# Token projections of a hybrid SSD and attention block: TensorE taken in source order, transposes one tile behind, the scan in three portions

## The chip, the cores and the metric

The kernel runs on one core of a Trainium2 chip. The metric is the device time of one execution in microseconds (us); lower is better. The engines are named as in the profile: PE is TensorE (matrix products and transposes), DVE is VectorE, ACT is ScalarE, POOL is GpSimd, SP is SyncE, which here only issues DMAs.

## The reference

Two layers over 256 context and 1024 latent tokens of width 1024 (10 tiles of 128 tokens). Each layer projects the normalised input once and splits the result between three branches:

```
p = split_proj((rmsnorm(h, g_pre) * (1 + sc) + sh)  w_in)   # xbc z dt | gq gk gv gg | dq dk dv dg
# A  SSD: conv on xbc, then a chunked scan forward and backward, chunks of 128
y_diag = einsum('bcqhn,bcshn,bchqs,bcshp->bcqhp', cc, bc, lmat, xd)
states = einsum('bcshn,bcsh,bcshp->bchpn', bc, decay_states, xd)
y_off  = einsum('bcqhn,bchpn,bcqh->bcqhp', cc, states_in, exp(a_cum))
y_s = rmsnorm((y_f + y_b + x * d_skip) * silu(z), norm_g)
# B  grouped-query attention: 4 query and 2 key heads of 64, rmsnorm and rotary on q and k
# C  differential attention: 8 query and 8 key heads of 32, rotary, 4 value heads of 64
h = h + gt * rmsnorm(concat([y_s, y_g * silu(gg), y_d * silu(dg)])  w_out, g_post)
```

The last layer drops the context's output.

## The kernel before, in words

All matrix products that need full precision are split: each operand is a high and a low part, and a product is three matmuls. Between the convolution and the attention of each layer lies the region that is touched here (about 206 to 602 us in the first layer, 1273 to 1625 us in the second).

**The token projections.** `tok_chunk` (L938 to L1000) runs five column chunks in the order 0 (gate z), 1 (differential q and k), 3 (differential v, 256 wide), 2 (grouped q, k, v, called gqa below), 4 (the attention's gate). A chunk loads 8 weight blocks (`wf`), splits them into `wh` and `wl` (9 buffers each), and then takes the 10 tiles of tokens. A tile is 8 blocks times 3 matmuls, 24 matmuls (L958, L959, L960) into one of two PSUM buffers `prj`. What follows a tile is by chunk: a gate (tanh, ACT, and one DVE step); or, for q and k, a copy `raw`, the norm `gqa_norm`, the rotary `rope`, the split `st` (L834 and L128), the transposes `qps` on PE (L841), a copy `tt` and the stores.

**The scan.** `scan` (L754) is a generator that walks the 10 chunks forward (`c`) and backward (`cb`). It is advanced beside chunks 0, 1 and 3, 1.3 portions for a tile that is 512 wide. `state_step` scales x on POOL (`xs`, L708), multiplies (`stp`, L714) and updates a state; `y_off` multiplies with the state (`po`, L726), and DVE scales the result into `yt` (L728). For each forward chunk a decay matrix is made in the buffer `ab` (16 DVE steps, `Exp`, 16 more steps, and a POOL product, L782), and its product is `pd` (L790). `ab`, `xs`, `yt` and `yp` have one buffer each.

**The finish.** `finish` (the gated norm with the transposes `ytp`, L744) runs beside chunks 2 and 4. `split_wout` prepares the output weights (`wos`) and stores them; some of these run before this region, the rest beside chunk 2.

**What sets the order.** The program is written in one order, and the framework then orders each engine's queue by a simulated timeline with priorities by position in the source. So PE's queue before is not the source's: an instruction that the timeline has not ready is put later, and matmuls of a following tile are taken first. Each engine then works strictly down its queue and waits on semaphores. SP issues nearly all DMAs in its queue's order, so a store that waits for its data holds the loads behind it.

The tables for the rotary (`cosg`, `sing`, and the products `Ckg`, `Cqg`, L930 and L931) are made at the start of the region.

Of the kernel before, what the change touches and what calls it, by code (L numbers as in the profile page):

```python
# [18 lines left out]
P = 128  # L19
KT = 8  # L20
# [47 lines left out]
def block_kernel(ctx: ExitStack, tc: tile.TileContext, tok, cvec, wmod, pack,  # L68
# [360 lines left out]
    for l in range(DEPTH):  # L429
# [275 lines left out]
        def state_step(c, dr, xb, S, first):  # L705

            xs = sp.tile([P, 2, 256], F32, name="xs", tag="xs")
# [14 lines left out]
        def y_off(c, dr, bc, S):  # L722

            po = xpp.tile([P, 2, 256], F32, name="po", tag="po")
            for g in range(2):
                TE.matmul(po[:, g], bc[g], S[:, g], start=True, stop=True)  # L726
            yt = sp.tile([P, 512], F32, name="yt", tag="yt")
            V.tensor_tensor(heads(yt), heads(po.rearrange("p g x -> p (g x)")), per_head(eacs, dr, c), op=ALU.mult)  # L728
            return yt

        def finish(c, fp, nb=2):
# [4 lines left out]
            SY.dma_start(zt, d_z[c])  # L736
            V.tensor_tensor(y, y, zt, op=ALU.mult)
# [3 lines left out]
            V.tensor_scalar(y, y, rr, None, op0=ALU.mult)  # L741
            pt = trp.tile([P, 4, P], F32, name="ytp", tag="tr")
# [9 lines left out]

        def scan():
# [3 lines left out]
            for c, cb in enumerate((1, 0, 9, 8, 7, 6, 5, 4, 3, 2)):  # L757
                xb = sp.tile([P, 2, 384], F32, name="xbf", tag="xb", bufs=2)
                SY.dma_start(xb, d_xb[c])
                if c >= t0:  # L760
                    ab = sp.tile([P, 2, 8, P], F32, name="ab", tag="ab")
                    SY.dma_start(ab, d_acs[:, c].unsqueeze(0).to_broadcast([P, 2, 8, P]))
                    bc = sp.tile([P, 4, P], F32, name="bct", tag="bct", bufs=2)
                    SY.dma_start(bc, d_bc[:, :, cs(c)].rearrange("i p t -> p i t"))
                    pg = xpp.tile([P, 2, P], F32, name="gp", tag="gp")
                    for g in range(2):
                        TE.matmul(pg[:, g], bc[:, 2 * g], bc[:, 2 * g + 1], start=True, stop=True)
                    gf = sp.tile([P, 2, 2, P], F32, name="gf", tag="gf")
                    V.tensor_tensor(gf[:, 0], pg, mge.unsqueeze(1).to_broadcast([P, 2, P]), op=ALU.mult)
                    V.tensor_tensor(gf[:, 1], pg, mle.unsqueeze(1).to_broadcast([P, 2, P]), op=ALU.mult)  # L770
                    D, W = ab[:, 0], ab[:, 1]
                    for h in range(8):
                        V.tensor_scalar(D[:, h], D[:, h], acs[:, 0, c, h:h + 1], None, op0=ALU.subtract)
                        V.scalar_tensor_tensor(D[:, h], W[:, h], acs[:, 1, c, h:h + 1], D[:, h],
                                               op0=ALU.subtract, op1=ALU.min)
                    S_.activation(D, D, AF.Exp)
                    yield
                    for h in range(8):
                        S_.activation(W[:, h], gf[:, 0, h // 4], AF.Copy, scale=dts[:, 0, c, h:h + 1])
                        V.scalar_tensor_tensor(W[:, h], gf[:, 1, h // 4], dts[:, 1, c, h:h + 1], W[:, h],  # L780
                                               op0=ALU.mult, op1=ALU.add)
                    G.tensor_tensor(W, W, D, op=ALU.mult)  # L782
                    y = sp.tile([P, 512], F32, name="y", tag="y", bufs=2)
                    G.tensor_tensor(y.rearrange("p (g h d) -> p g h d", g=2, h=4),
                                    xb[:, :, 0:256].rearrange("p g (h d) -> p g h d", h=4),
                                    pc("dskip").rearrange("p (g h) -> p g h", g=2).unsqueeze(3)
                                    .to_broadcast([P, 2, 4, 64]), op=ALU.mult)
                    pd = xpp.tile([P, 8, 64], F32, name="pd", tag="pd")
                    for h in range(8):
                        TE.matmul(pd[:, h], W[:, h], xb[:, h // 4, h % 4 * 64:h % 4 * 64 + 64],  # L790
                                  start=True, stop=True)
                    V.tensor_tensor(y, pd.rearrange("p h d -> p (h d)"), y, op=ALU.add)
                    if c:
                        yt = y_off(c, 0, (bc[:, 1], bc[:, 3]), Sf)
                        G.tensor_tensor(y, yt, y, op=ALU.add)
                    if c in half:
                        yt = sp.tile([P, 512], F32, name="yp", tag="yp")
                        SY.dma_start(yt, d_yp[c])
                        G.tensor_tensor(y, yt, y, op=ALU.add)
                    whole = c in half or c == 1  # L800
                    half.add(c)
                    SY.dma_start((d_ys if whole else d_yp)[c], y)
                    yield
                if c != NT - 1:
                    state_step(c, 0, xb, Sf, c == 0)
                xb = sp.tile([P, 2, 384], F32, name="xbb", tag="xb", bufs=2)
                SY.dma_start(xb, d_xb[cb])
                if c and cb >= t0:
                    ct = sp.tile([P, 2, P], F32, name="ct", tag="ct")
                    SY.dma_start(ct, d_bc.rearrange("(g b) p t -> b p g t", b=2)[1][:, :, cs(cb)])  # L810
                    yt = y_off(cb, 1, (ct[:, 0], ct[:, 1]), Sb)
                    if cb in half:
                        y = sp.tile([P, 512], F32, name="y", tag="y", bufs=2)
                        SY.dma_start(y, d_yp[cb])
                        G.tensor_tensor(y, yt, y, op=ALU.add)
                        SY.dma_start(d_ys[cb], y)
                    else:
                        half.add(cb)
                        SY.dma_start(d_yp[cb], yt)
                if cb != 2:  # L820
                    state_step(cb, 1, xb, Sb, c == 0)
                yield

# [85 lines left out]
        with pool("rot") as rp, pool("tokc", 2) as ck:  # L909
            rd = rp.tile([P, 3, 8, 16], F32, name="rd")  # L910
            cosd, sind, nsind = rd[:, 0], rd[:, 1], rd[:, 2]
            cosg = ck.tile([P, 8, 32], F32, name="cosg", tag="st", bufs=2)
            sing = ck.tile([P, 8, 32], F32, name="sing", tag="st", bufs=2)
            SY.dma_start(rd, roped.rearrange("a p t c -> p a t c"))
            SY.dma_start(cosg, ropeg[0])
            SY.dma_start(sing, ropeg[1])
            gain = {}
            for n, sc in (("qg", 64 ** -0.5), ("kg", 1.0)):
                gn = rp.tile([P, 64], F32, name=f"gn{n}")
                V.tensor_scalar(gn, pc(n), sc, None, op0=ALU.mult)  # L920
                gain[n] = gn

            tab = {}
            for n in ("kg", "qg"):
                c_ = rp.tile([P, 8, 2, 32], F32, name=f"C{n}")
                s_ = rp.tile([P, 8, 2, 32], F32, name=f"S{n}")
                for hf in range(2):
                    ga = gain[n][:, hf * 32:hf * 32 + 32].unsqueeze(1).to_broadcast([P, 8, 32])
                    gb = gain[n][:, 32 - hf * 32:64 - hf * 32].unsqueeze(1).to_broadcast([P, 8, 32])
# [692 lines left out]
```

## Times and profile before

| | us |
|---|---|
| three runs, median (lowest, highest) | 2074.26 (2069.14, 2074.6) |
| the profiled execution's own time | 2063.46 |
| its span | 2061.6 |
| PE busy | 1806.6 (88%) |
| DVE busy | 1428.5 (69%) |
| POOL busy | 1211.7 (59%) |
| ACT busy | 1041.5 (51%) |

The mean granted clock of PE over the span is 0.937. "Busy" is the union of the instructions on an engine; PE's matmuls overlap, so the time from one start to the next is the price of one. A bracket behind an instruction, [1.90 <-DVE th], is the idle time of its engine just ahead of it and what released it. In a window, idle PE is its length less its busy time, and a PEclk under 1.00 says that a part of it ran at the lower of the clock's two levels, 1.2 in place of 2.4 GHz.

### The profile page before, as it was taken

The page shows a single profiled execution, that of the slowest core. Times are in us where ns is not written, and L with a number is a line of the kernel's source. Part 1 is how long each engine was busy: PE and PEld are TensorE (multiplying, and loading weights), DVE is VectorE, ACT ScalarE, POOL GpSimd, SP SyncE. Part 2 cuts the span into 40 slices and gives each one's busy share as a digit, 9 for nine tenths or more (in the row PEclk, how much of TensorE's full clock was granted, in tenths as well). Part 3 has the DMA queues.
Part 4 walks back from the last instruction along what each step waited for, and adds up shares of the span by engine and source line. Part 5 has one row for each costly group of instructions (what it writes and reads, how often), then busy time and mean ns, then how long its engine had stood idle before and what let it go on. Part 6 is the DMA issues. An engine that isn't in the chain of part 4 may idle for free. (4 is left out here: it accounts for less than half of the span.)

```text
span 2061.6 us, 30333 instructions
## 1 busy us (share of the span) xinstructions
PE 1806.6 (88%) x9936; PEld 1471.4 (71%) x9936; DVE 1428.5 (69%) x3286; ACT 1041.5 (51%) x1955; POOL 1211.7 (59%) x1135
## 2 busy tenths in 40 slices
PE   4899989899879999988988799888899899989895
PEld 3677777787668667876775487777777777878783
DVE  4777566766538776698866578468656588788954
ACT  3445233334437775766654345234244477777661
POOL 3626245747616676777755326466567378787761
PEclk9899999899999999998989899999999999999897
DMA  9157546776786788786656138667766866557545
GB/s 290 47 170 271 152 165 191 236 235 176 222 259 198 245 263 257 234 256 202 211 191 214 63 102 280 226 183 231 244 202 204 260 185 192 157 155 237 161 152 205
DMA packets 359998, 418.57 MB, mean 203 GB/s; under 512 B 38753, under 2 KB 252833, under 8 KB 359841
## 3 DMA queue, kind: packets, MB, share of 16 engines
q1 hardware_dynamic: 359840, 416.64, 65.1%
q8 instruction: 78, 1.28, 0.3%
q14 instruction: 80, 0.65, 0.1%
HBM read 282.18 MB, written 134.38 MB: 202 GB/s over the span
## 5 line engine op out<-in xcount | busy, mean ns | idle before, releaser
L128 POOL TENSOR_TENSOR pl<-pf,ph 128x512 fp32r<-128x512 f32 x283 | 373.6, 1325 | 189.0 <-DVE ph L1391 69.7
L1241 DVE TENSOR_SCALAR_CACHE_REDUCE pt<-sc 128x512 f32<-128x512 f32 (+1 forms) x600 | 334.2, 587 | 78.5 <-PE sc L1239 63.4
L958 PE MATMUL prj<-wh,u 128*128 128x512 f32 (+1 forms) x768 | 296.6, 389 | 33.0 <-DVE th L964 18.1
L1254 ACT ACTIVATE pt<-pt,nm 128x1280 f32<-128x1280 f32 x192 | 262.3, 1366 | 92.1 <-DVE nm L1252 91.0
L959 PE MATMUL prj<-wl,u 128*128 128x512 f32 (+1 forms) x768 | 294.8, 384 | 10.3 <-POOL wl L128 7.8
L960 PE MATMUL prj<-wh,u 128*128 128x512 f32 (+1 forms) x768 | 291.7, 380 | 0.0
L1369 PE MATMUL tp<-ident,pt 128*128 128x128 f32 x1312 | 209.3, 285 | 14.0 <-ACT pt L1254 5.6
L1379 ACT COPY pf<-tp 128x512 f32<-128x512 f32 x289 | 166.8, 581 | 74.9 <-PE tp L1369 49.3
L1412 PE MATMUL po<-pl,vt 128*128 128x256 f32 x644 | 183.1, 307 | 15.6 <-POOL pl L128 14.7
L958 PEld LDWEIGHTS prj<-wh,u 128*128 128x128 f32 x768 | 151.8, 199 | 62.5 <-DVE th L964 19.9
L1411 PE MATMUL po<-ph,vt 128*128 128x256 f32 x644 | 186.0, 303 | 5.2 <-DVE ph L1391 2.9
L1369 PEld LDWEIGHTS tp<-ident,pt 128*128 128x128 f32 x1312 | 162.1, 147 | 37.9 <-ACT pf L1379 10.7
L959 PEld LDWEIGHTS prj<-wl,u 128*128 128x128 f32 x768 | 152.0, 198 | 38.0 <-POOL wl L128 11.2
L960 PEld LDWEIGHTS prj<-wh,u 128*128 128x128 f32 x768 | 151.7, 198 | 23.5
L1239 PE MATMUL sc<-dk,q 128*128 128x512 f32 (+1 forms) x400 | 146.1, 408 | 15.2 <-DVE pt L1241 12.0
L1412 PEld LDWEIGHTS po<-pl,vt 128*128 128x128 f32 x644 | 126.3, 196 | 33.0 <-POOL pl L128 25.3
L1411 PEld LDWEIGHTS po<-ph,vt 128*128 128x128 f32 x644 | 127.2, 197 | 19.4 <-DVE ph L1391 5.6
L606 DVE SCALAR_TENSOR_TENSOR cacc<-craw,hw,cacc 128x1284 f32<-128x1284 f32 (+1 forms) x64 | 120.0, 1877 | 28.0 <-ACT cacc L603 12.0
L581 PE MATMUL prj<-u,wTh 128*128 128x512 f32 x256 | 109.8, 429 | 22.2 <-DVE u L209 14.2
L1239 PE MATMUL sc<-gk,q 128*128 128x256 f32 (+1 forms) x400 | 110.0, 385 | 19.9 <-DVE pt L1241 16.7
L342 PE MATMUL ops<-y,wo 128*128 128x512 f32 (+1 forms) x304 | 117.7, 387 | 10.5 <-DMA y<-y 6.3
L582 PE MATMUL prj<-u,wTh 128*128 128x512 f32 x256 | 109.3, 427 | 7.4 <-DVE u L128 6.8
(277 smaller groups left out, 4310.7 us busy)
## 6 DMA issues: line engine op xcount, KB each, us to landing
wo<-wo SPq DMA_DIRECT2D x80, 512.0 KB, 4.9
wm<-in_wmod_dram SPq DMA_DIRECT2D x48, 512.0 KB, 6.2
dk<-dk SPq DMA_DIRECT2D x16, 1280.0 KB, 7.9
ab<-acs SPq DMA_DIRECT2D x18, 1024.0 KB, 7.5
wo<-wos SPq DMA_DIRECT2D x32, 512.0 KB, 3.7
wf<-in_wtok_dram SPq DMA_DIRECT2D x64, 256.0 KB, 4.4
y<-y SPq DMA_DIRECT2D x30, 512.0 KB, 5.7
op<-o SPq DMA_DIRECT2D x48, 256.0 KB, 4.4
```

The lines of the kernel that those rows point to most:

```text
L128: eng.tensor_tensor(out_, full, hi.bitcast(F32), op=ALU.subtract)
L606: V.scalar_tensor_tensor(acc[:, a0:1284], raw[:, a0 + j:1284 + j], hw[:, i * 5 + j:i * 5 + j + 1], acc[:, a0:1284], op0=ALU.mult, op1=ALU.add)
L958: TE.matmul(ps[:, c0:], uh, wh[k][:, c0:], start=k == 0, stop=False)
L959: TE.matmul(ps[:, c0:], uh, wl[k][:, c0:], start=False, stop=False)
L960: TE.matmul(ps[:, c0:], ul, wh[k][:, c0:], start=False, stop=k == KT - 1)
L1239: TE.matmul(ps[:, 0:b - a].rearrange("p (t c) -> p t c", c=P), q[:, jb.q0 + j], kt[:, a // P:b // P], start=x == 0, stop=x == len(qq) - 1)
L1241: V.tensor_scalar(ts[r][:, a:b], ps[:, 0:b - a], -1.0, None, op0=ALU.mult, op1=ALU.min, accum_out=mts[r][:, i:i + 1])
L1254: S_.activation(e, e, AF.Exp, bias=nm, scale=-1.0, accum_out=jb.s2[:, j, mp_:mp_ + 1])
L1369: TE.transpose(tp[:, j * P:(j + 1) * P], jb.pt[2 * hf + j % 2][:, cs(2 * s + j // 2)], ident)
L1379: S_.copy(pf[:, :w_], tp[:, :w_])
L1411: TE.matmul(o, vv, a[:, c], start=k == 0, stop=False)
L1412: TE.matmul(o, vv, b[:, c], start=False, stop=k == jb.nk - 1)
```

## The change

PE is taken out of the framework's ordering (`manual_schedule`) from ahead of the scan until chunk 4 and the last `finish` are done: its queue is then the source's order, while the other engines are still ordered by the timeline. With it the source's order is rewritten. The first two tiles of a chunk are interleaved block by block. The transposes of tile t (`turn`, kept in `behind`) are issued after the matmuls of tile t+1; `caught_up` empties the list ahead of the end of the scan and ahead of chunk 4. The scan has three portions a chunk: decay weights of `c` with the forward `y_off` and the result of the chunk before; the forward state; the backward `y_off` and state. Its loads are issued one chunk ahead, `ab` has two buffers, and `xs`, `yt` and `yp` share one tag of two buffers. `finish` has three portions, its transposes in the last. The rotary's tables are made at the start of chunk 2.

```diff
-            xs = sp.tile([P, 2, 256], F32, name="xs", tag="xs")
+            xs = sp.tile([P, 2, 256], F32, name="xs", tag="yt", bufs=2)
...
-            yt = sp.tile([P, 512], F32, name="yt", tag="yt")
+            yt = sp.tile([P, 512], F32, name="yt", tag="yt", bufs=2)
...
+        def load(c):
+                xf = sp.tile([P, 2, 384], F32, name="xbf", tag="xbf", bufs=2)
...
+                    ab = sp.tile([P, 2, 8, P], F32, name="ab", tag="ab", bufs=2)
...
+        def result(c, xf, W, y):
+            pd = xpp.tile([P, 8, 64], F32, name="pd", tag="pd")
...
+            V.tensor_tensor(y, pd.rearrange("p h d -> p (h d)"), y, op=ALU.add)
+            if c in half:
+                yp = sp.tile([P, 512], F32, name="yp", tag="yt", bufs=2)
...
+            for c, cb in enumerate(CB):
+                xf, ab, bc = ahead
+                if c >= t0:
+                    weights(c, ab, bc)
+                    y = skipped(c, xf, y_off(c, 0, (bc[:, 1], bc[:, 3]), Sf) if c else None)
+                back = load_back(c)
+                if left:
+                    result(*left)
+                yield
+                if c != NT - 1:
+                    state_step(c, 0, xf, Sf, c == 0)
+                    ahead = load(c + 1)
+                yield
+                xb, ct = back
+                if ct is not None:
+                    yb = y_off(cb, 1, (ct[:, 0], ct[:, 1]), Sb)
...
+                if cb != 2:
+                    state_step(cb, 1, xb, Sb, c == 0)
+                left = (c, xf, ab[:, 1], y) if c >= t0 else None
+                yield
+            result(*left)
...
+                    def turn():
+                        if not konly:
                             gq_out(ck, sf, t, trp_)
                         store_t(d_gk[:, :, cs(t)], qk_transpose(ck, sf, b0, 2, trp_)[:, 0:2])
+                behind.append(turn)
...
+                for group in [(first, first + 1)] + [(t,) for t in range(first + 2, NT)]:
...
+                    for k in range(KT + len(group) - 1):
+                        for i, t in enumerate(group):
+                            if 0 <= k - i < KT:
+                                product(pss[i], t, c0, k - i)
+                    todo_ = list(behind)
+                    behind.clear()
+                    for ps, t in zip(pss, group):
+                        tok_rows(ch, ps, t, c0)
+                        if todo_:
+                            todo_.pop(0)()
+                        yield
...
+            tok_order = ExitStack()
+            tok_order.enter_context(tc.manual_schedule(engines={mybir.EngineType.PE}))
...
+                caught_up()
                 for _ in sc:
                     pass
...
+                tables(rp2)
                 for t, _ in enumerate(tok_chunk(ck, 2, 0)):
...
+                    finish_on(fp, 2, t % 2 == 1)
+                caught_up()
+                while running:
+                    finish_on(fp, 2, False)
...
+            finish_end(ck, GNB)
+        tok_order.close()
```

What this does to PE's queue at the start of the region in the second layer: the transposes `xtp` are the last step of the convolution, `prj` is a projection matmul, `stp` the first state product of the scan. Before:

```order
L960 MATMUL prj<-wh,u_11553 128x512
L623 MATMUL xtp<-ident,cacc 128x128 x10
L958 MATMUL prj<-wh,u_11546 128x512
L959 MATMUL prj<-wl,u_11546 128x512
L960 MATMUL prj<-wh,u_11546 128x512
L958 MATMUL prj<-wh,u_11547 128x512
L959 MATMUL prj<-wl,u_11547 128x512
```

And now:

```order
L1072 MATMUL prj<-wh,u_11560 128x512
L623 MATMUL xtp<-ident,cacc 128x128 x10
L714 MATMUL stp<-xs,xbf 128x256 x2
L1070 MATMUL prj<-wh,u_11553 128x512
L1071 MATMUL prj<-wl,u_11553 128x512
L1072 MATMUL prj<-wh,u_11553 128x512
```

`stp` stood 62 projection matmuls behind the last `xtp`; now it stands right behind it, and those matmuls come after it.

At the end of the gqa chunk of the first layer, where the last tile's blocks are followed by chunk 4 (u_98 is the first block of a tile, u_105 its last). Before:

```order
L958 MATMUL prj<-wh,u_104 128x512
L959 MATMUL prj<-wl,u_104 128x512
L744 MATMUL ytp<-ident,yf 128x128 x4
L960 MATMUL prj<-wh,u_104 128x512
L958 MATMUL prj<-wh,u_105 128x512
L959 MATMUL prj<-wl,u_105 128x512
L960 MATMUL prj<-wh,u_105 128x512
L958 MATMUL prj<-wh,u_98 128x512
```

And now:

```order
L1071 MATMUL prj<-wl,u_105 128x512
L1072 MATMUL prj<-wh,u_105 128x512
L894 MATMUL qps<-identr,st 128x128 x6
L746 MATMUL ytp<-ident,yf 128x128 x4
L894 MATMUL qps<-identr,st 128x128 x6
L746 MATMUL ytp<-ident,yf 128x128 x4
L1070 MATMUL prj<-wh,u_98 128x512
```

Where transposes stood between matmuls of later tiles, each tile's six `qps` now follow the next tile's last matmul, and the last tile's stand ahead of every matmul of chunk 4.

In a middle chunk of the scan, first layer, PE (`po<-Sb` is the backward `y_off`, `stp<-xs,xbb` the backward state product). Before:

```order
L714 MATMUL stp<-xs,xbb 128x256 x2
L726 MATMUL po<-Sb,ct 128x256 x2
L960 MATMUL prj<-wh,u_102 128x512
L958 MATMUL prj<-wh,u_103 128x512
L959 MATMUL prj<-wl,u_103 128x512
L841 MATMUL qps<-identr,st 128x128 x8
L767 MATMUL gp<-bct 128x128
L790 MATMUL pd<-xbf,ab 128x64 x8
```

And now:

```order
L1072 MATMUL prj<-wh,u_105 128x512
L894 MATMUL qps<-identr,st 128x128 x8
L726 MATMUL po<-Sb,ct 128x256 x2
L714 MATMUL stp<-xs,xbb 128x256 x2
L803 MATMUL gp<-bct 128x128 x2
L726 MATMUL po<-Sf,bct 128x256 x2
L834 MATMUL pd<-xbf,ab 128x64 x8
```

POOL at the same place (`y<-yt,y` and `yp<-yt,yp` add a scaled `yt`; `raw` and `st` belong to the projections). Before:

```order
L784 TENSOR_TENSOR y<-xbf,pk_597 128x512
L708 TENSOR_TENSOR xs<-xbf,coef 128x512
L795 TENSOR_TENSOR y<-yt,y 128x512
L888 TENSOR_TENSOR raw<-raw,t_3220 128x512
L128 TENSOR_TENSOR st<-raw,st 128x8x32
L718 TENSOR_TENSOR Sf<-Sf,etot 128x512
L708 TENSOR_TENSOR xs<-xbb,coef 128x512
```

And now:

```order
L866 TENSOR_TENSOR yp<-yt,yp 128x512
L708 TENSOR_TENSOR xs<-xbb,coef 128x512
L718 TENSOR_TENSOR Sf<-Sf,etot 128x512
L827 TENSOR_TENSOR y<-yt,y 128x512
L817 TENSOR_TENSOR ab<-ab 128x1024
L708 TENSOR_TENSOR xs<-xbf,coef 128x512
L840 TENSOR_TENSOR y<-yp,y 128x512
```

On PE `po<-Sb` was followed by projection matmuls and transposes, and is now followed directly by the backward `stp`; on POOL the backward `xs` now stands directly behind the addition that frees a buffer of the shared ring.

## Rows read from the trace of the kernel before

**Rows 1.** Windows: us, busy (count) of PE, PEld, DVE, ACT, POOL; PEclk; DMA; GB/s
```profile
295.00:475.00 180.00, 157.14 (x847) 135.18 (x848) 119.14 (x271) 63.86 (x150) 105.48 (x85) 0.91 0.69 213
475.00:515.00 40.00, 37.87 (x191) 30.49 (x190) 24.57 (x51) 15.48 (x37) 29.25 (x38) 1.00 0.65 187
515.00:560.00 45.00, 38.53 (x178) 29.50 (x179) 28.42 (x51) 20.09 (x47) 32.85 (x41) 0.92 0.71 208
1345.00:1525.00 180.00, 154.12 (x883) 132.74 (x882) 124.55 (x279) 64.12 (x157) 111.35 (x99) 0.94 0.71 217
1525.00:1565.00 40.00, 36.95 (x176) 28.94 (x174) 22.03 (x45) 18.86 (x45) 29.99 (x41) 0.95 0.61 176
1565.00:1605.00 40.00, 38.93 (x180) 31.85 (x181) 23.22 (x40) 14.33 (x30) 21.89 (x26) 0.92 0.70 208
```

**Rows 2.** PE's waits, 295 to 475 us: who waited for whom, us, times, longest
```profile
PE prj L958 <- ACT raw L977: 5.4, 1, 5.4
PE po L726 <- DVE yt L728: 5.2, 2, 4.3
```

**Rows 3.** PE's waits, 1345 to 1525 us
```profile
PE po L726 <- DVE yt L728: 11.8, 6, 5.4
```

**Rows 4.** PE's timeline, gqa chunk and chunk 4, first layer: start, us, instruction
```profile
492.67 0.62 PE L841 MATMUL qps<-identr,st 128*128 128x128 f32 x6
...
575.22 0.39 PE L958 MATMUL prj<-wh,u 128*128 128x512 f32 x1
...
580.43 0.39 PE L960 MATMUL prj<-wh,u 128*128 128x512 f32 x1
```

**Rows 5.** PE's timeline, start of the region, first layer; a bracket is idle time before
```profile
218.38 1.55 PE L623 MATMUL xtp<-ident,cacc 128*128 128x128 f32 x10 [0.18 <-DVE cacc L610]
...
230.70 1.13 PE L714 MATMUL stp<-xs,xbf 128*128 128x256 f32 x4
234.64 1.22 PE L767 MATMUL gp<-bct 128*128 128x128 f32 x4 [2.81 <-DMA bct<-bc]
235.52 0.77 PE L958 MATMUL prj<-wh,u 128*128 128x512 f32 x1
...
240.36 0.43 PE L960 MATMUL prj<-wh,u 128*128 128x512 f32 x1
```

**Rows 6.** PE's timeline, start of the region, second layer
```profile
1287.86 0.73 PE L623 MATMUL xtp<-ident,cacc 128*128 128x128 f32 x4 [0.30 <-ACT xt L624]
...
1311.11 1.02 PE L714 MATMUL stp<-xs,xbf 128*128 128x256 f32 x4
```

**Rows 7.** POOL's timeline at the same place, second layer
```profile
1298.23 1.43 POOL L930 TENSOR_TENSOR Ckg<-cosg,gnkg 128x256 f32<-128x256 f32 x2 [2.68 <-DMA cosg<-in_ropeg_dram]
...
1301.20 1.47 POOL L128 TENSOR_TENSOR wos<-wof,wos 128x512 fp32r<-128x512 f32 x1
1307.58 1.05 POOL L708 TENSOR_TENSOR xs<-xbf,coef 128x512 f32<-128x512 f32 x1 [4.91 <-DMA xbf<-xb]
```

**Rows 8.** The tile yt: count, duration ns least/median/most, first and last start
```profile
L728 DVE TENSOR_TENSOR yt<-po,eacs x34: 675/680/694, 245.4 to 1510.0; 128x512 f32<-128x512 f32 x34
L815 POOL TENSOR_TENSOR y<-yt,y x9: 1270/1291/1612, 272.1 to 1512.8; 128x512 f32<-128x512 f32 x9
```

**Rows 9.** The line L708: the same columns
```profile
L708 POOL TENSOR_TENSOR xs<-xbb,coef x18: 1041/1086/2627, 236.4 to 1471.8; 128x512 f32<-128x512 f32 x18
```

**Rows 10.** ACT's timeline in the gqa chunk, second layer
```profile
1523.26 0.51 ACT L895 ACTIVATE gsq<-raw 128x384 f32<-128x384 f32 x1
...
1525.67 0.59 ACT L977 COPY raw<-prj 128x512 f32<-128x512 f32 x1 [1.50 <-PE prj L960]
...
1584.69 0.53 ACT L895 ACTIVATE gsq<-raw 128x384 f32<-128x384 f32 x1 [2.79 <-POOL raw L888]
```

**Rows 11.** POOL's timeline there: the last step of the same two tiles
```profile
1532.84 1.02 POOL L128 TENSOR_TENSOR st<-raw,st 128x384 fp32r<-128x384 f32 x1
...
1592.21 1.01 POOL L128 TENSOR_TENSOR st<-raw,st 128x384 fp32r<-128x384 f32 x1 [0.62 <-ACT st L834]
```

More of the change, by code (lines that the diff above doesn't have):

```diff
@@ L751, in finish, with finish_on, finish_end @@
                          yp.rearrange("p k a t -> p k (a t)").bitcast(F32))
+        running = []
+        def finish_on(fp, nb=2, new=True):
+            for g in list(running):
+                if next(g, 1):
+                    running.remove(g)
+            if new and todo:
+                running.append(finish(todo.pop(0), fp, nb))
+                next(running[-1])
+        def finish_end(fp, nb=2):
+            while running or todo:
+                finish_on(fp, nb, len(running) < nb)
         def scan():
@@ L777, in scan @@
[L777 to L795, printed above, removed]
@@ new lines, in skipped @@
+            def skipped(c, xf, yt):
+                y = sp.tile([P, 512], F32, name="y", tag="y", bufs=2)
+                G.tensor_tensor(y.rearrange("p (g h d) -> p g h d", g=2, h=4),
+                                xf[:, :, 0:256].rearrange("p g (h d) -> p g h d", h=4),
+                                pc("dskip").rearrange("p (g h) -> p g h", g=2).unsqueeze(3)
+                                .to_broadcast([P, 2, 4, 64]), op=ALU.mult)
+                if yt is not None:
+                    G.tensor_tensor(y, yt, y, op=ALU.add)
+                return y
@@ new lines, in result @@
+            def result(c, xf, W, y):
+                pd = xpp.tile([P, 8, 64], F32, name="pd", tag="pd")
+                for h in range(8):
+                    TE.matmul(pd[:, h], W[:, h], xf[:, h // 4, h % 4 * 64:h % 4 * 64 + 64],
+                              start=True, stop=True)
+                V.tensor_tensor(y, pd.rearrange("p h d -> p (h d)"), y, op=ALU.add)
+                if c in half:
+                    yp = sp.tile([P, 512], F32, name="yp", tag="yt", bufs=2)
+                    SY.dma_start(yp, d_yp[c])
+                    G.tensor_tensor(y, yp, y, op=ALU.add)
+                whole = c in half or c == 1
+                half.add(c)
+                SY.dma_start((d_ys if whole else d_yp)[c], y)
@@ new lines, in scan @@
+            ahead = load(0)
+            left = None
+            for c, cb in enumerate(CB):
[14 more added lines that the diff above has]
+                    yb = y_off(cb, 1, (ct[:, 0], ct[:, 1]), Sb)
@@ L812, in scan @@
                     if cb in half:
[L813 to L816, printed above, removed]
+                        yp = sp.tile([P, 512], F32, name="yp", tag="yt", bufs=2)
+                        SY.dma_start(yp, d_yp[cb])
+                        G.tensor_tensor(yp, yb, yp, op=ALU.add)
+                        SY.dma_start(d_ys[cb], yp)
@@ L923, in block_kernel @@
[L923 to L929, printed above, removed]
-                    G.tensor_tensor(c_[:, :, hf, :], cosg, ga, op=ALU.mult)
-                    V.scalar_tensor_tensor(s_[:, :, hf, :], sing, -1.0 if hf == 0 else 1.0, gb,
-                                           op0=ALU.mult, op1=ALU.mult)
-                tab[n] = (c_, s_)
+            gain, tab = {}, {}
```

205 lines of the change are left out of this document (111 added, 94 removed).

## The prediction

> **What bounds the kernel now.** I read the page's engine shares first: PE is busy for 88% of the span, so the time is PE's work plus its holes plus what it runs at the lower clock. Then the windows [rows 1]: in the scan's stretch of the first layer (295 to 475 us) PE is idle for 180 - 157.1 = 22.9 us and its granted clock is 0.91, which is 0.09 x 180 = 16 us lost; in the second layer (1345 to 1525) 25.9 us idle and 0.06 x 180 = 11 us of clock. In the gqa chunk (475 to 515, 1565 to 1605) PE is nearly full: 37.9 and 38.9 of 40 us. So the scan's stretch has something to win, about 39 + 37 us, and the gqa chunk has almost nothing. Then the waits of the scan's stretch: the largest are one wait of 5.4 us for the copy `raw`, and `po` waiting for `yt`, 5.2 us in the first layer [rows 2] and 11.8 us in the second [rows 3]. They are what PE's order and the single buffers can act on. Last come the timelines, for prices. A projection matmul costs the distance of two starts: 24 of a tile go from 575.22 to 580.43, 5.21 / 23 = 0.227 us, so 5.45 us a tile [rows 4]. After the wait of 2.81 us for `gp` the next 12 projection matmuls start from 235.52 to 240.36, 4.84 / 11 = 0.44 apart: the lower level, 11 x 0.21 = 2.4 us lost [rows 5]. That is my price of one fall of the clock.
>
> The change adds no PE instruction worth counting: the same products and transposes are put in another order. So every term is a wait that goes or comes.
>
> **Start of the region: +7 and +11 us.** In the first layer `xtp` ends at 219.9 and `stp` starts at 230.7 [rows 5]. Between them PE did 30 projection matmuls, 30 x 0.227 = 6.8 us, and then waited 2.81 us for the DMA of `gp`. Now `stp` stands right behind `xtp`, with nothing between. What it needs (`xs` on POOL, from a load) comes no sooner, since nothing on that path is moved; so `stp` still starts at 231, `gp` at 234.6, and the 30 matmuls remain to be done: +6.8, call it 7. The slow matmuls after that wait are paid in both. Bounds: 0 if `xs` comes as soon as `xtp` ends, 11 if the whole distance from 219.9 to 230.7 is added. In the second layer 62 matmuls stood ahead of `stp`, 62 x 0.227 = 14.1 us of the 22.5 us between 1288.6 and 1311.1 [rows 6]. Here `xs` can come sooner: it waits for the load of `xbf`, which is issued behind the store of the `wos` that POOL makes at 1301.20, after the rotary's table products that begin at 1298.23 [rows 7]. These products move to chunk 2, about 2.8 us, so `xs` comes at 1304.8 and `stp` at about 1305.9. Then come `stp` (1.0) and the 62 matmuls, with one fall of the clock after the wait: 1305.9 + 1.0 + 14.1 + 2.4 = 1323.4, against 1311.1 + 1.0 = 1312.1 before: +11. Bounds: nothing if the loads ahead bring `xs` before `xtp` ends, which the 4.91 us of POOL's wait for that load [rows 7] would have to allow, and +25 if both wait twice as long.
>
> **The scan beside chunks 0, 1 and 3: -12 us a layer, -24.** What goes: the wait for `raw`, since transposes that are one tile behind no longer hold PE's queue; most of `po` waiting for `yt` (two buffers); the waits for `ab` (two buffers, loaded a chunk ahead); and some of the lower clock that followed them: 5.4 + 5.2 + some 5 of smaller waits and 10 of the 16 us of clock, about -26 in the first layer, and as much in the second, where 11.8 us of `yt` stand for more and the clock for less. What comes: `xs`, `yt` and `yp` now share two buffers. In the chunks in which the backward result is added to a partial one, `xs` has to wait until POOL has added the `yt` that occupies its buffer, and that `yt` is made from the `po` directly ahead of `stp` in PE's queue. So PE waits there for DVE's 0.68, POOL's 1.29 [rows 8] and `xs` itself, 1.09 [rows 9], with three handovers 3.4 us, in three or four chunks a layer: 12. Where a tile advances the scan by two portions (the 1.3 of the credit) nothing lies between two such steps, for which I add 2. Net -12. Bounds: -38 a layer if all idle time and lost clock of [rows 1] goes, +15 if the returns also cost the clock each time and the old waits only change their name. I stay in the middle, since old and new waits have rows of like size.
>
> **The gqa chunk: +18 and +22 us.** The chain from a tile's last matmul to the end of its `st`: `raw` 0.59, then `gsq` to the end of `st`. One tile goes from 1523.26 to 1532.84 + 1.02 = 10.6 us, another from 1584.69 to 1592.21 + 1.01 = 8.5 [rows 10, 11]; with the copy and a handover 9.5 to 11.6, and I take 10.5. Before, the matmuls of one or two further tiles were put ahead of the transposes, and the chain was covered: PE was full [rows 1]. Now the transposes of tile t must come directly after tile t+1's matmuls, and nothing of tile t+2 may pass them. PE has 5.45 us of matmuls, 0.62 of `qps` [rows 4] and on average 0.2 of `ytp` in a tile, about 6.3. Two tiles and one chain make a cycle: tile t+2's matmuls start after the transposes of t, so two tiles take 10.5 + 6.3 = 16.8, 8.4 each: 2.1 us of wait a tile, for the 8 tiles with a rotary 17 us. At the end nothing of chunk 4 covers the last tile's chain: 10.5 less the 0.6 and the handover of the transposes before it, about 9. With 3 us of lower clock, 29. Against it stand holes of before at the chunk's edges that need not be added again: in 515 to 560 us 6.5 us idle and 0.08 x 45 = 3.6 of clock, in 1525 to 1565 3.0 and 2.0, and 3.2 of clock behind it [rows 1]. So +18 and, with 7 given back, +22. Bounds: if the framework's order on DVE and POOL brings the chain down to 8 us, the cycle is 7.2 a tile, 7 + 7 + 3 - 11, so +6 and +10; with 12 us and three slow matmuls in each tile it is +35 each.
>
> Here the Trainium skill speaks against the change. The windows show short holes both ways: 2.1 us of idle time in 475 to 515 left the clock at 1.00, and the 3.0 us in 1525 to 1565 went with 0.95 and then 0.92 [rows 1]; after the 2.81 us at 234.64 it had fallen [rows 5]. "TensorE: Matmul & The Clock Gate", section "HAM oscillation — how this bites in real kernels", has it that a loop whose engine waits in each round falls to the lower clock in each and pays again and again. By that each wait of 2.1 us would be followed by slow matmuls; it is the third rival.
>
> **The rest: 0.** Loads ahead, the longer tag and the interleaved first pair cost no engine time; the pair's second tile hides the arrival of the weight blocks, which the chunk edges above include. In chunk 4 what waits now waits as before, as the attention's loads stand in SP's queue ahead of the gate's store in both orders. The attention is ordered anew by the framework: 0, within ±10.
>
> **Sum.** 18 - 24 + 40 = +34 us on the profiled execution's 2063.5, 2097.5. The median of the runs is 2074.3, 10.8 above that execution, so 2108 where runs are compared. The likeliest case's own range, from the middle of the bounds, is 2085 to 2135.
>
> **The rivals.** (1) Faster: PE's order was the cause of the holes in the scan, and the ring of two buffers does not bind since POOL has the partial result added in time. Then -30 a layer there, +18 at the start (the rows for it are plain), and the gqa chunk near its lower bound, +16: -26, 2048. For it: 22.9 and 25.9 us idle in the scan's windows; against it: the gqa chunk was full. It decides at a chain of about 8 us. (2) Gains and losses cancel: 2074, with the scan at -26 a layer and the rest as I sum it. (3) Slower than I say: each gqa wait costs the clock, 16 tiles x 2.4 = 38 us more: 2146. It needs the clock to fall after waits of 2 us, for which the rows are divided. Were the order not kept at all, nothing would move: the queue shows that it is.
>
> **How the numbers follow.** Forecast 0.50, rival 1 0.25, rival 2 0.12, rival 3 0.13. The measurement can tell about 0.3%, 6 us, from no change. Rival 1 gives 0.25 faster, with 0.02 from the edge of rival 2; 0.10 within 0.3%; the rest, 0.63, slower. The range: 2042 to 2142 takes in most of rival 1, which centres at 2048, and about half of rival 3.
>
> **What would show it.** In the trace after: PE idle ahead of the first `stp` of each layer, about 11 and 17 us, released by POOL's `xs`; PE ahead of `qps` in the gqa chunk waiting for POOL's `st`, some 2 us a tile, and one wait of about 9 us ahead of chunk 4; ahead of backward `stp` waits of 3 us for `xs`; no wait of `prj` for `raw` and almost none of `po` for `yt` in the scan. I am wrong if the gqa chunk's `st` comes within 7 us, if the scan's windows lose more than 30 us of holes, or if the new holes carry no loss of time because PE's later work shrinks.

## The result and the profile after

The changed kernel takes 2268.21 us (median of 4 runs, 2261.39 to 2268.92) against 2071.7 us for the kernel before (median of 4 runs): a ratio of 1.0946, 95% interval 1.091 to 1.0982. It is 196 us slower. The forecast was 2108 us with a range up to 2142, so the sign was right and the size (+34 us) was too small by a factor of about six. Two executions in this document ran far longer than the others of their kernel (5414 us in an experiment below, 2206 us of the kernel before), and medians and ratios leave them out.

The profiled execution has a span of 2267.1 us and a mean granted clock of 0.900 (0.937 before). The page shows the same work and more holes:

```profile
span 2267.1 us, 30282 instructions
PE 1834.0 (81%) x9936; PEld 1492.1 (66%) x9936; DVE 1435.8 (63%) x3286; ACT 1041.5 (46%) x1955; POOL 1201.2 (53%) x1135
```

PE's instructions are 9936 as before and its busy time is 27 us longer. The span grew by 205.5 us. The table of PE's waits over the whole span (who waited for whom, us, times, longest) says for whom PE stood still:

```profile
PE stp L714 <- POOL xs L708: 109.4, 15, 17.9
PE qps L894 <- POOL st L128: 73.7, 14, 12.8
PE stp L714 <- issue: 27.6, 5, 8.2
```

Before, the waits in the two stretches of the scan had `yt` and `raw` at their head with 5.2, 11.8 and 5.4 us [rows 2, 3]; the waits for `raw` are gone and those for `yt` are down to one of 2.0 us, as forecast. In their place are 137 us of `stp` and 74 us of `qps`, more than the whole loss. By stage, PE's windows (length, then busy time of PE, PEld, DVE, ACT, POOL, granted clock, DMA share, GB/s) from the last `xtp` to the end of the scan, from there to the attention, and both again for the second layer:

```profile
218.40:525.20 306.80, 215.66 (x1050) 182.05 (x1051) 165.15 (x363) 73.33 (x173) 123.45 (x97) 0.82 0.51 155
525.20:715.80 190.60, 140.25 (x629) 113.62 (x628) 65.26 (x128) 52.16 (x116) 75.35 (x98) 0.86 0.56 165
1393.70:1657.60 263.90, 186.92 (x994) 160.63 (x994) 150.81 (x306) 67.48 (x157) 116.25 (x95) 0.84 0.55 172
1657.60:1818.80 161.20, 116.27 (x517) 94.78 (x515) 54.60 (x115) 44.86 (x101) 68.46 (x92) 0.84 0.59 170
```

Idle PE is 91 us in the first and 77 us in the third window; over a shorter stretch of before it was 22.9 and 25.9 us [rows 1]. DVE is busy for at most 57% of these windows, POOL for 44% and ACT for 28%: no engine is the bound, PE waits for answers. What one such wait looks like in the scan, in the timeline of all engines (SPq is a DMA issue on SP):

```profile
410.53 2.04 PE L726 MATMUL po<-Sb,ct 128*128 128x256 f32 x4
412.60 0.40 SPq L796 DMA_DIRECT2D ct<-bc  x1
412.61 0.69 DVE L728 TENSOR_TENSOR yt<-po,eacs 128x512 f32<-128x512 f32 x1 [1.22 <-PE po L726]
413.09 1.84 SPq L905 DMA_DIRECT2D dq<-tt  x4
415.02 1.24 SPq L905 DMA_DIRECT2D dk<-tt  x2
416.36 0.62 SPq L865 DMA_DIRECT2D yp<-yp  x1
...
420.00 1.26 POOL L866 TENSOR_TENSOR yp<-yt,yp 128x512 f32<-128x512 f32 x1 [2.75 <-DMA yp<-yp]
421.34 1.04 POOL L708 TENSOR_TENSOR xs<-xbb,coef 128x512 f32<-128x512 f32 x1
422.44 2.08 PE L714 MATMUL stp<-xs,xbb 128*128 128x256 f32 x4 [9.87 <-POOL xs L708]
```

`yt` is ready at 413.3, as I had priced it. But the addition that frees its buffer needs `yp` as well, whose load is issued at 416.36, behind the load of `ct`, which waited for `po` to have read its one buffer, and behind six stores of the projections. It lands at 420.0. The step that I priced at 3.4 us takes 9.87. A second kind does not end with the ring:

```profile
284.28 1.02 PE L714 MATMUL stp<-xs,xbf 128*128 128x256 f32 x4
...
285.14 1.03 PE L726 MATMUL po<-Sb,ct 128*128 128x256 f32 x4
...
287.89 2.05 DVE L809 TENSOR_SCALAR ab<-ab,acs 128x128 f32<-128x128 f32 x6 [4.97 <-DMA ab<-acs]
...
290.82 1.09 POOL L708 TENSOR_TENSOR xs<-xbb,coef 128x512 f32<-128x512 f32 x1
...
293.49 0.68 DVE L720 TENSOR_TENSOR Sf<-stp,Sf 128x512 f32<-128x512 f32 x1
...
294.27 2.05 PE L714 MATMUL stp<-xs,xbb 128*128 128x256 f32 x4 [8.10 <-issue]
```

Here a tile advanced two portions, so the forward `stp`, `po` and the backward `stp` stand in a row. `xs` is done at 291.9, but `stp` has one PSUM buffer, and DVE, which reads the forward result (`Sf`), has the next chunk's decay steps ahead of it and waits 4.97 us for their load. `stp` starts when `Sf` ends, at 294.2; the profile has no releaser for it ("issue"). Without that hold-up `stp` could have started at 291.9, when `xs` was done, so only 2.4 of these 8.1 us hang on `Sf` alone.

In the gqa chunk, the transposes on PE (first), then ACT and POOL of two tiles:

```profile
553.24 0.70 PE L894 MATMUL qps<-identr,st 128*128 128x128 f32 x6 [2.25 <-POOL st L128]
556.07 1.00 PE L894 MATMUL qps<-identr,st 128*128 128x128 f32 x6 [2.13 <-POOL st L128]
...
564.94 0.63 PE L894 MATMUL qps<-identr,st 128*128 128x128 f32 x6
...
578.43 1.00 PE L894 MATMUL qps<-identr,st 128*128 128x128 f32 x6 [6.92 <-POOL st L128]
...
586.46 0.62 PE L894 MATMUL qps<-identr,st 128*128 128x128 f32 x6
...
599.70 1.00 PE L894 MATMUL qps<-identr,st 128*128 128x128 f32 x6 [6.70 <-POOL st L128]
```
```profile
565.14 0.59 ACT L1027 COPY raw<-prj 128x512 f32<-128x512 f32 x1 [3.85 <-PE prj L1072]
...
566.56 0.55 ACT L948 ACTIVATE gsq<-raw 128x384 f32<-128x384 f32 x1
...
571.55 0.58 ACT L1027 COPY raw<-prj 128x512 f32<-128x512 f32 x1 [3.93 <-PE prj L1072]
...
575.77 0.63 ACT L740 ACTIVATE zt<-yf 128x512 f32<-128x512 f32 x1 [3.31 <-DVE yf L738]
...
576.40 0.51 ACT L948 ACTIVATE gsq<-raw 128x384 f32<-128x384 f32 x1
576.82 0.49 ACT L887 CAST st<-raw 128x384 fp32r<-128x384 f32 x1
```
```profile
567.69 1.29 POOL L128 TENSOR_TENSOR yp<-zt,yp 128x512 fp32r<-128x512 f32 x1 [0.47 <-ACT yp L750]
...
577.39 0.99 POOL L128 TENSOR_TENSOR st<-raw,st 128x384 fp32r<-128x384 f32 x1
```

From the copy `raw` at 565.14 to the end of `st` at 578.4 it is 13.2 us, where I read 9.5 to 11.6 from the rows of before [rows 10, 11]. Steps of `finish` (`yp`, `zt`) stand between the tile's own in the queues of POOL and ACT; `zt` made ACT wait 3.31 us for DVE, which had waited for the load of `z`, and the split `st` came behind it. The next tile has its hold-up elsewhere: its copy `raw` is done at 572.1, but its `gsq` starts only at 576.4. Two tiles take 599.70 - 578.43 = 21.3 us, and each of the two waits of 6.9 and 6.7 us is followed by slow transposes, 1.00 us for six in place of 0.62 or 0.63.

### The profile page after: what moved, and what is told of

Same layout as the page of the kernel before. It is cut to its first block, busy times and chain, and to the rows that moved or that the text cites. A ratio compares the mean times of both kernels' runs of the same rounds, so it can differ in the third digit from the quotient of the medians.

```text
span 2267.1 us, 30282 instructions
## 1 busy us (share of the span) xinstructions
PE 1834.0 (81%) x9936; PEld 1492.1 (66%) x9936; DVE 1435.8 (63%) x3286; ACT 1041.5 (46%) x1955; POOL 1201.2 (53%) x1135
## 5 line engine op out<-in xcount | busy, mean ns | idle before, releaser
L1070 PE MATMUL prj<-wh,u 128*128 128x512 f32 (+1 forms) x768 | 309.3, 403 | 18.2 <-DVE th L1015 15.2
L1072 PE MATMUL prj<-wh,u 128*128 128x512 f32 (+1 forms) x768 | 293.4, 382 | 0.0
L1509 PE MATMUL po<-pl,vt 128*128 128x256 f32 x644 | 183.8, 308 | 23.7 <-POOL pl L128 20.3
L1070 PEld LDWEIGHTS prj<-wh,u 128*128 128x128 f32 x768 | 158.8, 207 | 46.6 <-DVE th L1015 16.7
L1466 PEld LDWEIGHTS tp<-ident,pt 128*128 128x128 f32 x1312 | 159.4, 145 | 32.1 <-ACT pf L1476 9.6
L1071 PEld LDWEIGHTS prj<-wl,u 128*128 128x128 f32 x768 | 157.5, 205 | 32.9 <-DVE wl L128 4.7
L1072 PEld LDWEIGHTS prj<-wh,u 128*128 128x128 f32 x768 | 156.1, 203 | 26.6
L1336 PE MATMUL sc<-dk,q 128*128 128x512 f32 (+1 forms) x400 | 144.5, 410 | 17.9 <-DVE pt L1338 10.7
L606 DVE SCALAR_TENSOR_TENSOR cacc<-craw,hw,cacc 128x1284 f32<-128x1284 f32 (+1 forms) x64 | 119.2, 1863 | 27.7 <-ACT cacc L603 21.3
L581 PE MATMUL prj<-u,wTh 128*128 128x512 f32 x256 | 107.8, 421 | 22.6 <-DVE u L209 14.1
L714 PE MATMUL stp<-xs,xbb 128*128 128x256 f32 x72 | 34.1, 624 | 111.7 <-POOL xs L708 84.1
L1336 PE MATMUL sc<-gk,q 128*128 128x256 f32 (+1 forms) x400 | 110.2, 380 | 15.1 <-DVE pt L1338 11.8
```

The source lines that it names most:

```text
L1070: TE.matmul(ps[:, c0:], uh, wh[k][:, c0:], start=k == 0, stop=False)
L1071: TE.matmul(ps[:, c0:], uh, wl[k][:, c0:], start=False, stop=False)
L1072: TE.matmul(ps[:, c0:], ul, wh[k][:, c0:], start=False, stop=k == KT - 1)
L1336: TE.matmul(ps[:, 0:b - a].rearrange("p (t c) -> p t c", c=P), q[:, jb.q0 + j], kt[:, a // P:b // P], start=x == 0, stop=x == len(qq) - 1)
L1466: TE.transpose(tp[:, j * P:(j + 1) * P], jb.pt[2 * hf + j % 2][:, cs(2 * s + j // 2)], ident)
L1509: TE.matmul(o, vv, b[:, c], start=False, stop=k == jb.nk - 1)
```

## The experiments

Each is timed against the kernel before on its own chip (2063 to 2066 us there). The changed kernel, 1.0946, is the other end. The kernel before took 2071.7 us beside that one. So where two runs are compared that were not timed on one chip, the difference is that of their ratios times 2065 us, and it is certain to some 10 us.

**Free order for PE, all else as changed.** The edit:

```diff
-            tok_order.enter_context(tc.manual_schedule(engines={mybir.EngineType.PE}))
```

> The changed kernel with one thing undone: PE's queue is ordered by the framework's timeline again, while scan, transposes, buffers and loads are written as in the changed kernel. Theory A (PE's fixed order does the harm: the same instructions with nothing that may pass a waiting one): nearly all of the 196 us come back, 2050 to 2100 us. Rival B (the new source does the harm by itself: one ring of two buffers for xs, yt and yp, loads and decay steps a chunk ahead on SP and DVE): 2150 us or more also with a free order.

Measured: 2064.26 us, 0.9991 (0.9972 to 1.0011). Theory A holds: with this source the fixed order costs the 196 us, and the new source as a whole costs nothing that can be measured where the framework orders PE. Its windows over the same stages hold the same number of projection matmuls as those of the changed kernel:

```profile
214.50:437.50 223.00, 195.81 (x1051) 168.13 (x1050) 171.80 (x362) 72.19 (x173) 118.84 (x96) 0.95 0.69 211
437.50:592.00 154.50, 133.18 (x628) 107.92 (x627) 71.76 (x129) 52.04 (x117) 78.86 (x99) 0.94 0.72 210
1284.90:1498.10 213.20, 185.12 (x994) 159.82 (x993) 152.34 (x306) 66.70 (x157) 118.03 (x96) 0.90 0.68 215
1498.10:1612.40 114.30, 106.98 (x516) 87.44 (x516) 55.71 (x114) 42.49 (x101) 69.89 (x91) 0.97 0.70 206
```

Stage by stage the fixed order costs 83.8, 36.1, 50.7 and 46.9 us, 217.5 in all; idle PE accounts for 179 of them (the lengths less PE's busy time: 263 against 84), and the other 38 are busy time (659 against 621) for the same instructions, at a granted clock of 0.82 to 0.86 in place of 0.90 to 0.97. The whole spans differ by 205 us: some 12 us come back outside these windows, where the stretch between the layers' windows is 15 us shorter in the changed kernel.

**Fixed in one part only.** In the first, `tok_order` is closed when the scan ends; in the second it is opened there.

```diff
                 for _ in sc:
                     pass
+            tok_order.close()
             sc_.close()
...
-        tok_order.close()
```

> The changed kernel, but PE's order is fixed only until the scan has ended; chunks 2 and 4 are ordered by the framework again. From the traces, the stretch up to the scan's end costs 79 + 54 us more than before at equal numbers of projection matmuls, and the stretch behind it 34 + 44. If the two parts are independent: 2268 - 78 = 2190 us. If the waits in the gqa chunk come from the scan's lateness and not from the fixed order: 2250 us or more.

> The changed kernel, but PE's order is fixed only from the start of the gqa chunk to the end of chunk 4; the scan's stretch is ordered by the framework. If the parts are independent: 2268 - 133 = 2135 us, with the waits of qps for POOL's st (37.9 and 34.8 us) unchanged. If the scan's new source costs as much with a free order: 2200 us or more.

Measured: 2193.91 us, 1.0615 (1.0586 to 1.0643), and 2148.48 us, 1.0385 (1.0351 to 1.0418). The two parts cost 128 and 83 us. They add up to 211, where both at once cost 195 (0.0946 of 2065): within the uncertainty they are independent, and the scan's part is the larger. With the second part alone, the waits of `qps` for POOL's `st` stay, 35.8 and 32.1 us.

**The ring and the place of `stp` in the scan.** Own buffer for `xs`; the backward `y_off` moved ahead of the second `yield`; both.

```diff
-            xs = sp.tile([P, 2, 256], F32, name="xs", tag="yt", bufs=2)
+            xs = sp.tile([P, 2, 256], F32, name="xs", tag="xs")
```

> The changed kernel with xs in a buffer of its own, so that only yt and yp share the ring of two. Theory R (the ring: xs has to wait for the addition that frees its buffer): the waits of stp for POOL's xs (52.5 and 56.8 us) go, with the clock behind them some 120 us, 2150 us. Rival P (the place: stp stands directly behind po or the other stp in PE's queue, and DVE's 16 decay steps for the next chunk stand ahead of the yt and Sf that it needs): xs comes sooner but stp still waits 5 to 8 us a chunk for the state's PSUM buffer, 2220 to 2260 us.

> The changed kernel with the backward y_off moved ahead into the second portion, right behind the forward state step, so that the backward stp stands a portion (mostly a tile of projections) behind the po whose yt it waits for; the shared ring stays. Theory P (stp's place in PE's queue): PE does projections while DVE and POOL answer, most of the 72 and 65 us of stp waits go except where a tile advances two portions, 2180 to 2200 us. Rival R (the ring alone, and the loads and decay steps ahead of yt on DVE): the same waits fall on the next instruction, above 2240 us.

> Both edits in one: xs in a buffer of its own and the backward stp a portion later. With xs alone 2185 us were measured, and its trace still has 25.6 us and 10.5 us of stp waiting (for the state's PSUM buffer, which DVE reads late). If place and ring are two causes of the same waits: 2145 us (2185 less 36 and a little clock). If the ring was the only cause that counts: 2185 us.

Measured: own buffer 2184.62 us, 1.0565 (1.053 to 1.06); later place 2220.13 us, 1.0768 (1.0737 to 1.08); both 2184.45 us, 1.0592 (1.0559 to 1.0625). The ring alone is worth 79 us, about six tenths of the scan's part, though less than the 120 of theory R. The later place alone is worth 37; 2220 us lies between the two statements. Both together are worth 73, no more than the ring alone: both edits cure the same waits, and P as a second cause falls. With `xs` in its own buffer PE's waits in the first layer's scan are

```profile
PE stp L714 <- issue: 25.6, 6, 7.8
PE gp L803 <- DMA bct<-bc: 8.5, 1, 8.5
PE qps L894 <- DVE st L884: 7.6, 2, 4.0
```

so the waits for `xs` are gone there (52.6 us in the changed kernel), and those of the second kind are left.

**The transposes two tiles behind, and all three edits.**

```diff
-                    todo_ = list(behind)
-                    behind.clear()
+                    lag = 1 if ch == 2 else 0
+                    todo_ = behind[:max(0, len(behind) - lag)]
+                    del behind[:len(todo_)]
```

> The changed kernel with the gqa chunk's transposes two tiles behind in place of one, everything else kept. Theory L (the wait is the latency of the chain from a tile's last matmul to its st against one tile of matmuls): 26 and 22 us of qps waits go, the last one ahead of chunk 4 (11.5 and 12.8) stays, with the clock some 65 us: 2205 us. Rival Q (ACT, DVE and POOL cannot finish a tile's chain in 6 to 7 us): the waits stay as they are, 2250 us or more.

> PE's order still fixed, with all three edits: xs in its own buffer, the backward stp a portion later, the gqa transposes two tiles behind. If these three are all that the fixed order lacks: 2268 less 84 (measured for xs), less 40, less 65: 2080 us, within 25 us of before. What is left then would be the start (8.5 and 17 us) and the wait ahead of chunk 4 (11.5 and 12.8 us), each with its clock. If the fixed order itself, anywhere, is the trouble: 2120 us or more.

Measured: 2235.24 us, 1.0834 (1.0801 to 1.0868), and 2158.79 us, 1.0477 (1.0446 to 1.0508). The first is worth 23 us, less than half of the 63 that theory L gave, so neither statement holds whole. PE's waits for `st` fall from 37.9 to 25.2 us in the first layer, and most of the rest sits at the end of the chunk. PE's timeline of the kernel with this edit alone:

```profile
603.56 1.00 PE L894 MATMUL qps<-identr,st 128*128 128x128 f32 x6 [5.16 <-POOL st L128]
614.15 1.00 PE L894 MATMUL qps<-identr,st 128*128 128x128 f32 x6 [8.71 <-POOL st L128]
620.41 1.00 PE L894 MATMUL qps<-identr,st 128*128 128x128 f32 x6 [5.26 <-POOL st L128]
```

In the middle the latency is covered (waits of 0.6 to 2.2 us); the last three tiles now wait ahead of chunk 4, with nothing behind them that may pass. ACT's timeline of the same kernel shows that rival Q has a part in this:

```profile
582.16 0.52 ACT L948 ACTIVATE gsq<-raw 128x384 f32<-128x384 f32 x1 [0.38 <-POOL raw L941]
590.10 0.53 ACT L948 ACTIVATE gsq<-raw 128x384 f32<-128x384 f32 x1 [3.17 <-POOL raw L941]
598.93 0.52 ACT L948 ACTIVATE gsq<-raw 128x384 f32<-128x384 f32 x1 [1.11 <-POOL raw L941]
```

Each tile's `gsq` waits for POOL's rotary step of the tile before (in the source they share two buffers), and a tile comes every 8.4 us, while its work on PE takes about 6.3. So the chains fall behind PE, and the last tiles pay for it. Whether more buffers would speed them up was not tested. The three edits together leave 95 us, not 25. The fixed order keeps costing in places that no single edit reaches.

**DVE in source order too.** With `engines={PE, DVE}`, once on the changed kernel and once with the three edits.

> The changed kernel with DVE's queue in the source's order too, so that the next chunk's decay steps, which wait for the load of ab, can no longer stand ahead of the yt, Sf and Sb that PE's stp waits for. Theory D (stp's waits without the ring are DVE's queue: the reader of the state's PSUM buffer stands behind those steps): the 19.3 and 8.2 us of stp waits without a named releaser go and the waits for xs shrink, 2200 to 2235 us. Rival (a fixed order on DVE only moves the hold-up to the projections' own steps, rope and split, which then wait behind the scan's): 2268 us or more.

> The three edits (xs in its own buffer, backward stp a portion later, gqa transposes two tiles behind) with PE and DVE in the source's order. They gave 2159 us with PE alone fixed; its trace has 22.1 and 9.9 us of stp waits without a named releaser, at half clock behind them. Theory D: 2110 to 2135 us. Rival: DVE's own order costs as much as it gives, 2150 us or more.

Measured: 2354.04 us, 1.1389 (1.1364 to 1.1415), and 2259.32 us, 1.0941 (1.0911 to 1.097). Both went the rival's way, 91 and 96 us slower than with PE alone. With the three edits PE's waits from 205 to 620 us show why:

```profile
PE po L726 <- DVE yt L728: 33.6, 8, 9.5
PE ytp L746 <- DVE yf L742: 22.7, 5, 5.6
PE prj L1071 <- DVE wl L128: 20.1, 5, 9.7
PE gp L803 <- DMA bct<-bc: 8.7, 1, 8.7
PE stp L714 <- issue: 7.8, 2, 7.1
```

The waits of the second kind did fall (22.1 us to 7.8), so DVE's queue has a part in them, but its fixed order makes larger ones elsewhere.

**Loads a portion earlier.** `ahead = load(c + 1)` moved ahead of the first `yield`: once with PE fixed, `xs` in its own buffer and the later place (2184.45 us without the earlier loads), and once with all three edits and a free order.

> PE's order fixed, xs in its own buffer and the backward stp a portion later (2184 us), and the loads of the next chunk issued a portion earlier, before the forward state step in place of behind it. In the trace without this, DVE waits 24.7 us in the first layer for the load of ab with Sf, which frees the state's PSUM buffer, queued behind it, and stp waits 21.9 us without a named releaser. Theory D' (the load of ab is late, and DVE's queue passes the delay on to stp): DVE's wait for ab and most of stp's 21.9 and 9.9 us go, 2145 to 2160 us. Rival (stp waits for something else there): 2184 us, stp's waits unchanged even where DVE's wait for ab has gone.

> All three edits and the earlier loads, every engine's queue ordered by the framework (2053 us without the earlier loads). Where nothing is held in a fixed order the late load is passed by other work, so 2053 us within 0.4%; if the scan's stretch is set by that load also under a free order, 2035 to 2045 us.

Measured: 2188.26 us, 1.0582 (1.0546 to 1.0618), and 2052.09 us, 0.9917 (0.9882 to 0.9952). The first decides nothing: DVE waits 23.5 us for the load of `ab` after the edit and 23.7 before it, since the load stays behind the `pd` that frees its buffer, so what was to be taken away is still there. Whether that load is what holds `stp` stays open. The second makes no difference to the three edits with a free order (2052.94 us, reported last), as was expected where other work passes the late load.

**Old source, PE fixed.**

> The kernel before with nothing changed but PE's queue, which is fixed to its own source's order over the same stretch: each tile's transposes right behind its own matmuls, the scan's old portions. Theory A (the fixed order is the cost and the rewritten source is there to limit it): a full chain of 8 to 13 us ahead of the transposes of each of 20 tiles of q and k a layer, 40 x 9 = 360 us, and the scan's waits besides, 2450 to 2600 us. Rival (the old source stands the fixed order better than the new one): below 2268 us.

Measured: 2487.49 us, 1.2046 (1.2016 to 1.2077), as theory A had it. PE's waits over the span:

```profile
PE qps L841 <- POOL st L128: 184.7, 22, 12.3
PE qps L841 <- DVE st L831: 118.0, 18, 11.3
```

Forty waits, 303 us, 7.6 each. So the rewritten source is worth 227 us under a fixed order, and nothing under a free one (0.9991).

**A version that beats both.** The three edits with no fixed order.

> The same three edits with every engine's queue ordered by the framework. If a free order hides what the edits change, as it hid the new source (0.999 of before): 2064 us within 0.5%. If the shared ring still costs something under a free order: 2045 to 2055 us, a version that beats both.

Measured: 2052.94 us, 0.9933 (0.9915 to 0.9951) of before, 0.7% faster, in the range that was given for a ring that still costs something. The interval excludes no change, and the run with the earlier loads besides came out the same on another chip (0.9917). Which of the three edits brings it was not separated, so that it is the ring is not shown.

## Why the prediction came out as it did

**The sign and the reason were right.** PE adds no work, so each term is a wait that comes or goes. PE's waits for `raw` and `yt` went, and `stp`, `qps` and the start got new ones, in the places named. The waits for `ab` did not go where they are largest: DVE waits 30.0 us for that load in the first layer before and 30.1 after, and in the second 15.5 and 10.4.

**The start: right in size.** The first layer waits 8.7 us there (11 forecast), though `gp` comes first and its load releases it, not `xs`; the first `stp` of the second layer waits 17.9 (17 forecast).

**The scan: the step that failed.** The stage from the last `xtp` to the end of the scan holds the start and the scan. They were forecast at +7 - 12 = -5 and +11 - 12 = -1 us and came to +84 and +51, stage against stage with the free order. That is 140 of the 171 us which the forecast lacks. What failed is the term for the returns: 3.4 us of `stp` waiting in three or four chunks a layer, and 2 us for tiles that advance two portions.

- The price. In the four chunks of the first layer and three of the second in which `stp` follows such an addition, it waits 39.9 and 28.9 us, 8.6 to 12.0 each time. I had added the durations of `yt`, the addition and `xs` with handovers, as if each queue were free for them. In six of these seven POOL's addition waits for the load of `yp`, in the case shown above issued behind a blocked load and six stores; in the seventh `yt` stands behind the next chunk's decay steps on DVE.
- The number. The other waits of `stp` in the scan come to 32 and 18 us, where I had 2. Those read above and beside it arise where a tile advances two portions, and where the state's PSUM buffer is read late because `Sf` stands behind the decay steps.
- The clock. I kept the price of its fall out of this term and even counted 10 us of clock in the first layer as won. The granted clock over the first layer's stage is 0.82, against 0.95 with the free order, and the same instructions keep PE busy 20 us longer there.

That the shared ring decides most of this was named rightly: its removal is worth 79 of the 128 us that the fixed order costs up to the scan's end.

**The gqa chunk: mechanism right, chain mis-sized.** I took 10.5 us for the chain; it is 13.2, so two tiles take 21.3 us and not 16.8 (13.2 and 8.1 for a tile's work on PE, which I had at 6.3 and which now begins at the lower clock). In the tile that sets this pace the steps of `finish` lengthen the part from `gsq` on to 11.8 us; it was 8.5 to 10.6 in [rows 10, 11]. A second slip was to set `gsq` right behind the copy, though [rows 10] show it waiting 2.79 us for the tile before. That is the 4.3 us which the next tile loses in the changed kernel, in part, and the pace of 8.4 us with the transposes two tiles behind. In the kernel before, the copies `raw` of the two tiles that I read are

```profile
1519.89 0.59 ACT L977 COPY raw<-prj 128x512 f32<-128x512 f32 x1 [0.40 <-POOL irm L123]
...
1565.71 0.59 ACT L977 COPY raw<-prj 128x512 f32<-128x512 f32 x1 [0.22 <-POOL st L128]
```

and from them to the end of `st` it is 14.0 and 27.5 us. PE was full all the same, because later matmuls went ahead. The waits at the end of the chunk, forecast at 9 us, are 11.5 in the first layer and 12.8 and 5.9 in the second, there for the last two tiles with no projection matmul between them; the splits of chunk 4's weights (`wl`, four of 1.26 us on POOL in the second layer) stand among these tiles' steps. The forecast of +18 and +22 was +36 and +47 for the stage from the scan's end to the attention.

**The third rival came nearest, and its reason was only partly there.** It gave 2146 us and needed the clock to fall after waits of 2 us. In the first layer's gqa chunk the wait of 2.25 us left the clock at 1.00 (six transposes in 0.70 us); the one of 2.13 right behind it was followed by 0.50 (1.00 us). After the waits of 6.7 to 11.5 us the clock was 0.50 each time, which agrees with "TensorE: Matmul & The Clock Gate", section "HAM oscillation — how this bites in real kernels", in the Trainium skill. The prediction stretched that section to shorter waits than those it describes. The idle time itself was 179 of the 217 us, and no rival had that.

**The first rival fell.** It needed a chain of about 8 us and a ring that does not bind, and the traces show 13.2 us and a ring worth 79. Whether the framework's order caused the holes of before in the scan is not shown: with a free order and the new source PE is still idle for 27 us of the first stage (22.9 in the shorter window of [rows 1]), at the same total time.

## What to carry to other kernels

In a fixed order PE paid the latency of every answer that it asked for, less the work that stood between question and answer. That latency was not the sum of the durations of its steps: read it with what stands ahead of each step in the other engines' queues, DMA issues included, and count two consecutive questions on one buffer as one chain. In the gqa chunk the chain took 13.2 us, and the source offered 5.5 us of matmuls against it. Offering two tiles of them removed a third of the waits (37.9 to 25.2 us), since the other engines also took longer for a tile (8.4 us) than PE (6.3): so compare rates as well as latencies. Before a scheduler is overruled, it pays to run the new source under it: that run alone separated the two halves of this change.

## What the runs showed that was not expected

Two causes of one wait do not add: the own buffer and the later place are worth 79 and 37 us alone and 73 together. Fixing a second engine's order cured two thirds of what it was aimed at (22.1 to 7.8 us in the first layer) and cost 96 us. And a rewritten source that made no difference under the framework's order (0.9991) was worth 227 us under a fixed one.
